# A decoder layer with 32 experts: the order of the last weight loads, and the final gate's product in split float32r terms

## The chip, the cores and the metric

The kernel runs on one core of a Trainium2 chip. The metric is device time of one launch in microseconds (us): 1184.36 us for the kernel before, the median of 3 runs (1183.37 to 1185.8). A lower number is better.

## The reference, cut to what matters

One decoder layer over 256 tokens of width 1024, all in float32. The change touches the last expert's second product and the last line, the gated embedding.

```python
D_MODEL = 1024; SEQ = 256; N_EXPERTS = 32; TOP_K = 4
h = x + mixer(rms_norm(x)) @ w_out                 # attention and recurrence, not touched here
m = rms_norm(h, ffn_norm_g)
for e in range(N_EXPERTS):                         # mixture of experts, added to h
    gu = m @ w_gu[e] + b_gu[e]                     # 1024 x 2048 weights
    gate = jnp.minimum(gu[:, :D_EXPERT], 7.0)
    up = jnp.clip(gu[:, D_EXPERT:], -7.0, 7.0)
    y = ((up + 1.0) * gate * jax.nn.sigmoid(1.702 * gate)) @ w_down[e] + b_down[e]
    out = out + gates[:, e:e + 1] * y              # gates is zero but for a token's four experts
h = h + out
h = h + (p @ W_ple) * jax.nn.sigmoid(h @ W_ple_gate)   # 256 x 1024 by 1024 x 1024
```

## The kernel before, in words

**The stream.** All large weights come through one list, `seq`, in pieces of 1 MB. SyncE (SP) issues one DMA for each piece, strictly in the order of the list (`fill`, L172), as soon as a buffer of the pool "slots" is free. For expert e the list holds eight pieces of gate-and-up weights ("GU", 128 rows x 2048 columns) and four of down weights ("D", two blocks of 128 x 1024). D of expert e-1 stands behind GU of expert e. At the end of the list stand GU of expert 31, D of expert 30, the four pieces of the final gate ("pg", four blocks of 128 x 512, in the order `GATE = [(0, 0), (1, 0), (0, 1), (1, 1)]` of column half and row half), and last D of expert 31:

```python
    expert("D", E - 2)
    for n, hf in GATE:
        add(("pg", n), hf, p_gate, 512 * n)
    expert("D", E - 1)
```

A piece is taken out by `need` and its buffer given back by `used`. Pieces of the mixer's weights are split on arrival into a high and a low float32r part (`split`: a ScalarE copy that rounds, L193, and a subtraction on VectorE or GpSimd, L194), and their products are three float32r matmuls (L380 to L382: high x high, low x high, high x low). GU, D and pg are used as they are, in float32; the trace has two matmul records for each of those matmuls.

**The experts.** Every expert has room for 64 tokens. `gate_up` (L1016) multiplies each GU piece as it lands; `hidden` transposes the result; `down` (L1047) multiplies each D piece as it lands, four matmuls of 64 x 512 a piece, for both column halves side by side on the array; ScalarE copies the sum out (`y`, L1051); `scatter` (L1058) adds it to the 256 tokens' accumulators `acc`, four matmuls. For expert 31 there is a function of its own, `last_down` (L1118, L1122): column half by column half, and inside one half in an order that takes rows of the first and the third D piece in turn, then of the second and the fourth.

**The end.** `final` adds `acc` to `h` (VectorE, L1129), transposes `h` with 128 x 128 matmuls (L1134), and ScalarE copies them to `fT` (L1135). `gate` multiplies `fT` with the pg pieces, 32 float32 matmuls of 128 x 512 (L1152). For each of the four output blocks of 128 x 512 follow a sigmoid (ScalarE, L1157), a product with the projected embedding `pp` (VectorE, L1158), a sum with `h` (L1159) and the DMA to the output (L1160), each in two halves of 256 columns.

The program is ordered by a scheduler with a timeline model, so instructions of one engine can stand in another order than the source has them; each engine then runs its own queue strictly in that order.

Of the kernel before, what the change touches and what calls it, by code (L numbers as in the profile page):

```python
# [11 lines left out]
F32 = mybir.dt.float32  # L12
F32R = mybir.dt.float32r
# [3 lines left out]
AF = mybir.ActivationFunctionType  # L17
OP = mybir.AluOpType
X = mybir.AxisListType.X

D = 1024
T = 256
E = 32
# [7 lines left out]
GATE = [(0, 0), (1, 0), (0, 1), (1, 1)]  # L31
# [5 lines left out]
def constants():  # L37
    P = np.arange(128)
    ident = np.eye(128, dtype=np.float32)
    t = np.arange(256)  # L40
    dl = t[:, None] - t[None, :]
    c = ((dl >= 0) & (dl <= 128)).astype(np.float32)
    for dil in (4, 16):
        c += ((dl >= 0) & (dl % dil == 0)).astype(np.float32)
    logc = np.where(c > 0, np.log(np.maximum(c, 1.0)), NEG).astype(np.float32)
    am = np.concatenate([logc[:128, :128], logc[128:]], axis=1)
    hm = []
    for L in (64, 32, 16, 8, 4, 2, 1):
        s, q = P[:, None], P[None, :]
        hm.append((s // (2 * L) == q // (2 * L)) & (s % (2 * L) < L) & (q % (2 * L) >= L))  # L50
    hm.append(P[:, None] == P[None, :])
    hm = np.concatenate([m.astype(np.float32) for m in hm], axis=1)
    tri = (P[:, None] < P[None, :]).astype(np.float32)
    half = 8
    inv = (500000.0 ** (-np.arange(half, dtype=np.float32) / np.float32(half))).astype(np.float32)
    inv = np.broadcast_to(inv, (128, 8))
    slot = np.broadcast_to(np.tile(np.arange(1, 65, dtype=np.float32), 2), (128, 128))
    sel = np.zeros((128, 32, 2), np.float32)
    for k in range(128):
        sel[k, k % 32, (k // 32) % 2] = 1.0  # L60
    sel = sel.reshape(128, 64)
    scan = np.ones((128, 1024), np.float32)
    scan[:, ::64] = 0.0
    parts = dict(ident=ident, inv=inv, am=am, hm=hm, tri=tri, slot=slot, sel=sel, scan=scan)
    at, off = {}, 0
    for n, a in parts.items():
        at[n] = (off, a.shape[1])
        off += a.shape[1]
    return at, np.ascontiguousarray(np.concatenate([np.asarray(a, np.float32) for a in parts.values()], axis=1))
# [41 lines left out]
def layer(ctx, tc, A, at):  # L111
    nc = tc.nc
    pe, act, dve, pool, sp = nc.tensor, nc.scalar, nc.vector, nc.gpsimd, nc.sync

    pers = ctx.enter_context(tc.tile_pool(name="pers", bufs=1))
    S = Slots(ctx.enter_context(tc.tile_pool(name="slots", bufs=N_SLOTS)), N_SLOTS)
# [8 lines left out]
    def add(name, hf, w, c=0):  # L125
        seq.append((name, hf))
        src[name, hf] = w[:, 4 * hf:4 * hf + 4, c:c + 512]
# [11 lines left out]
    def expert(kind, e):  # L139
        w, n = (w_gu, 8) if kind == "GU" else (w_dn, 4)  # L140
        for j in range(n):
            seq.append(((kind, e), j))
            src[(kind, e), j] = w[e, j]

    for e in range(E):
# [3 lines left out]
        if e == E_PLE:  # L149
            seq.append(("pj", 0))  # L150
            src["pj", 0] = A["ple_proj"][0].rearrange("(j p) n -> p j n", p=128)
    expert("D", E - 2)
    for n, hf in GATE:
        add(("pg", n), hf, p_gate, 512 * n)
    expert("D", E - 1)
    place = {k: i for i, k in enumerate(seq)}
    st = {"next": 0, "raw": 0, "cap": 0, "split": 0, "keep": 0}
    raw, parts, owner = {}, {}, {}
# [20 lines left out]
    def native(k):  # L179
        return k[0] == "pj" or k[0][0] in ("GU", "D", "pg")  # L180
# [17 lines left out]
    def ahead(name, hf, n):  # L198
        i = place[name, hf]
        while st["split"] < min(i + 1 + n, len(seq)):  # L200
            split(seq[st["split"]])
            st["split"] += 1

    def need(name, hf):
        ahead(name, hf, 0)
        r = parts.pop((name, hf))
        if native((name, hf)):
            owner[name, hf] = r[1]
        return r

    def used(name, hf, n=1):
        if native((name, hf)):
            S.free(1, owner.pop((name, hf)))
        st["raw"] -= 1
        ahead(name, hf, n)
        fill()


    h = S.new([128, 2, D], F32, "h")
# [50 lines left out]
    def bank():  # L270
        return ps.tile([128, 512], F32, name="bk", bufs=4)

    mm = misc = bank

    def pz():
        return ps.tile([128, 1024], F32, name="pz", bufs=2)
# [44 lines left out]
    for j in range(0, 8, 2):  # L321
        b = bank()
# [4 lines left out]
        for jj in range(2):  # L327
            s = b[:, jj * 256:jj * 256 + 256]
# [448 lines left out]
    for k in range(4):  # L777
        for g in range(2):
            c = g * D + (k % 2) * 512
# [47 lines left out]
    wp = ctx.enter_context(tc.tile_pool(name="work", bufs=1))  # L827
    R = {e: {} for e in range(E)}
    bgu = wp.tile([128, D], F32R, name="bgu")
    halves = (slice(0, 64), slice(64, 128))  # L830
# [174 lines left out]
    def gate_up(e, between):  # L1005
        G, U = mm(), mm()
        x = R[e]["x"]
        for k, P in enumerate((G, U)):
            pe.matmul(P, R[e]["sel"], bgu[:, k * 512:k * 512 + 512], start=True, stop=False,  # L1009
                      skip_group_check=True)  # L1010
# [28 lines left out]
    def down(e):  # L1039
        P = mm()  # L1040
        t = R[e]["h"]
        for j in range(4):
            w, _ = need(("D", e), j)
            for k in range(2):
                f = 2 * j + k
                for n in range(2):
                    pe.matmul(P[halves[n], :], t[:, f % 4, f // 4, :], w[:, k, n * 512:n * 512 + 512], start=f == 0, stop=f == 7,  # L1047
                              skip_group_check=True)
            used(("D", e), j, 0)
        y = wp.tile([128, 512], F32, name="y", bufs=2)  # L1050
        act.activation(y, P, AF.Copy)  # L1051
        R[e]["y"] = y

    def scatter(e):
        t, y = R[e]["ST"], R[e]["y"]
        for tt in range(2):
            for n in range(2):
                pe.matmul(acc[tt][n], t[halves[n], tt * 128:tt * 128 + 128], y[halves[n], :], start=e == 0, stop=False, skip_group_check=True)  # L1058

    acc2 = [pz(), pz()]  # L1060
    acc = [[acc2[n][:, tt * 512:tt * 512 + 512] for n in range(2)] for tt in range(2)]
# [13 lines left out]
    for e in range(E):  # L1075
# [22 lines left out]
        if e == E_SPILL:  # L1098
            overflow()
            st["keep"] -= 3  # L1100
            fill()
    scatter(E - 2)


    fT = S.new([128, 8, T], F32, "fT")
    sgs = S.new([128, 4, 512], F32, "sgs")

    def last_down(n):

        P = mm()  # L1110
        t = R[E - 1]["h"]
        for c in range(4):
            for k in range(2):
                f = 4 * k + c
                if (f // 2) not in last:
                    last[f // 2], _ = need(("D", E - 1), f // 2)
                w = last[f // 2]
                pe.matmul(P[halves[k], :], t[:, c, k, :], w[:, f % 2, n * 512:n * 512 + 512], start=c == 0, stop=c == 3, skip_group_check=True)  # L1118
        y = wp.tile([128, 512], F32, name="y", bufs=2)
        act.activation(y, P, AF.Copy)  # L1120
        for tt in range(2):
            pe.matmul(acc[tt][n], R[E - 1]["ST"][:, tt * 128:tt * 128 + 128], y, start=False, stop=True, skip_group_check=True)  # L1122

    last = {}

    def final(n):
        c = slice(n * 512, n * 512 + 512)
        for tt in range(2):
            dve.tensor_tensor(h[:, tt, c], h[:, tt, c], acc[tt][n], OP.add)  # L1129
        for j in (4 * n, 4 * n + 2):  # L1130
            b = misc()
            for k in range(2):
                for tt in range(2):
                    pe.transpose(b[:, k * 256 + tt * 128:k * 256 + tt * 128 + 128], h[:, tt, (j + k) * 128:(j + k) * 128 + 128], ident)  # L1134
            act.activation(fT[:, j:j + 2, :].rearrange("p j t -> p (j t)"), b, AF.Copy)  # L1135

    zp = {}

    def gate(n, hf):
        if not hf:  # L1140
            if n:
                zp[n] = [mm(), mm()]
            else:
                t = pz()
                zp[n] = [t[:, 0:512], t[:, 512:1024]]
        p = zp[n]
        w, _ = need(("pg", n), hf)
        for tt in range(2):
            s = slice(tt * 128, tt * 128 + 128)
            for jj in range(4):  # L1150
                j = 4 * hf + jj
                pe.matmul(p[tt], fT[:, j, s], w[:, jj, :], start=j == 0, stop=j == 7)  # L1152
            if hf:
                for c0 in range(0, 512, 256):
                    c = slice(n * 512 + c0, n * 512 + c0 + 256)
                    sg = sgs[:, 2 * n + tt, c0:c0 + 256]
                    act.activation(sg, p[tt][:, c0:c0 + 256], AF.Sigmoid)  # L1157
                    dve.tensor_tensor(sg, sg, pp[:, tt, c], OP.mult)  # L1158
                    dve.tensor_tensor(sg, sg, h[:, tt, c], OP.add)  # L1159
                    sp.dma_start(A["out"][0, tt * 128:tt * 128 + 128, c], sg)  # L1160

    last_down(0)
    last_down(1)
    final(0)
    final(1)
    for n, hf in GATE:
        gate(n, hf)


_INS = ["x", "p", "positions", "mix_norm_g", "w_in", "q_norm_g", "k_norm_g", "hgrn_lb_logits", "hgrn_norm_g", "w_out",  # L1170
# [20 lines left out]
```

## Time and profile before

| | us |
|---|---|
| median of 3 runs | 1184.36 |
| the profiled execution, whole time | 1185.23 |
| its span, first to last instruction | 1183.4 |
| DMA, mean over the span | 365 GB/s |
| PE busy (matmuls) | 1094.4 (92%) |
| VectorE busy | 284.0 (24%) |
| ScalarE busy | 195.1 (16%) |
| granted TensorE clock, mean | 0.98 |

The kernel moves 432 MB and spends most of its span on that: in the slices of the page between 240 us and 1125 us most show 415 to 418 GB/s. The time outside those slices is the mixer at the start and the tail after the last weights, and the change is all in the tail. Times below are us from the start of the span. PE is TensorE's matmuls, PEld its weight loads, ACT ScalarE, DVE VectorE, SPq SyncE's queue of DMA issues; "1.00" and "0.50" in a clock column are the 2.4 and the 1.2 GHz level.

### The profile page before, as it was taken

How to read it: one execution, taken by the hardware profiler on the slowest of the kernel's cores; microseconds unless marked ns; L12 is line 12 of the kernel's file. 1: busy time of each engine (PE TensorE's matmuls, PEld its weight loads, DVE VectorE, ACT ScalarE, POOL GpSimd, SP SyncE). 2: the span in 40 equal slices, each digit the busy share in tenths (PEclk: the TensorE clock that was granted, in tenths of full speed). 3: DMA queues.
4: the chain of work that ended last, by engine and by line, in shares of the span. 5: the costliest groups of instructions: out<-in, count | busy, mean ns of one | idle time of the engine just before them, and what ended most of it. 6: DMA issues, size and time to landing. Idle time of an engine off the chain costs nothing. (4 is left out here: it accounts for less than half of the span.)

```text
span 1183.4 us, 12240 instructions
## 1 busy us (share of the span) xinstructions
PE 1094.4 (92%) x4969; PEld 448.5 (38%) x4969; DVE 284.0 (24%) x601; ACT 195.1 (16%) x359; POOL 73.8 (6%) x77
## 2 busy tenths in 40 slices
PE   5899989999999999999999999899999999998778
PEld 4778764333333333333333322233333332222223
DVE  4878652211121111111112111001111211110001
ACT  5656531001010000000001000010001100000001
POOL 4432230000000000000000000000000000000000
PEclk9989997999999999999999999999999999999979
DMA  9913668999999999999999999999989999999941
GB/s 308 344 48 107 229 251 321 389 416 415 418 417 416 417 418 416 417 416 417 418 417 417 416 417 418 408 417 417 416 330 419 417 416 418 416 416 418 407 179 35
DMA packets 87117, 432.41 MB, mean 365 GB/s; under 512 B 7736, under 2 KB 9184, under 8 KB 54288
## 3 DMA queue, kind: packets, MB, share of 16 engines
q1 hardware_dynamic: 86480, 430.35, 90.1%
q0 software_dynamic: 576, 1.23, 0.4%
q8 instruction: 40, 0.66, 0.2%
q14 instruction: 21, 0.17, 0.0%
HBM read 430.51 MB, written 1.05 MB: 365 GB/s over the span
## 5 line engine op out<-in xcount | busy, mean ns | idle before, releaser
L1016 PE MATMUL bk<-raw,x 128*64 128x512 f32 x2048 | 476.1, 599 | 12.5 <-DMA raw<-in_expert_w_gate_up 12.3
L1016 PEld LDWEIGHTS bk<-raw,x 128*64 128x64 f32 x2048 | 143.5, 137 | 313.1 <-issue 264.3
L1047 PE MATMUL bk<-raw,ht 128*64 128x512 f32 x992 | 239.7, 598 | 10.4 <-DMA raw<-in_expert_w_down 10.3
L1047 PEld LDWEIGHTS bk<-raw,ht 128*64 128x64 f32 x992 | 69.0, 137 | 143.8 <-issue 112.2
L1023 DVE TENSOR_SCALAR gm<-bk 128x512 f32<-128x512 f32 x32 | 22.1, 691 | 365.2 <-PE bk L1016 365.2
L1024 ACT ACTIVATE sgm<-gm 128x512 f32<-128x512 f32 x32 | 20.2, 630 | 423.0 <-DVE gm L1023 423.0
L846 PE MATMUL bk<-h,sx 128*64 128x512 f32 x256 | 66.3, 616 | 9.5 <-ACT st L1002 9.5
L997 DVE TENSOR_SCALAR sg<-c_slot,posx,gates 128x128 f32<-128x128 f32 x64 | 19.3, 343 | 213.4 <-PE bk L1000 213.4
L1058 PE MATMUL pz<-y,st 64*128 64x512 f32 x248 | 64.6, 632 | 3.3 <-PEq L947 1.9
L838 POOL CAST sb<-c_sel 128x128 fp32r<-128x128 f32 x32 | 9.3, 293 | 848.6 <-PE bk L1009 834.2
L194 POOL TENSOR_TENSOR lo<-raw,hi 128x1024 fp32r<-128x1024 f32 x20 | 49.1, 2472 | 85.7 <-ACT hi L193 85.7
L859 DVE TENSOR_TENSOR x<-bk,gcol 128x256 f32<-128x256 f32 x64 | 24.2, 419 | 109.3 <-PE bk L855 109.3
L193 ACT ACTIVATE hi<-raw 128x1024 fp32r<-128x1024 f32 x36 | 37.8, 1056 | 23.5 <-issue 9.8
L1051 ACT ACTIVATE y<-bk 128x512 f32<-128x512 f32 x31 | 18.5, 597 | 134.2 <-PE bk L1047 134.2
L380 PE MATMUL pz<-hi,ahi 128*128 128x512 f32 x80 | 33.9, 423 | 6.5 <-DVE N L608 6.2
L1058 PEld LDWEIGHTS pz<-y,st 64*128 64x128 f32 x248 | 22.4, 192 | 44.8 <-issue 41.6
L835 DVE TENSOR_SCALAR sx<-c_slot,posx,rstd 128x64 f32<-128x64 f32 x64 | 17.2, 312 | 80.1 <-PE bk L846 80.0
L848 ACT ACTIVATE xr<-bk 128x512 f32<-128x512 f32 x32 | 19.1, 597 | 94.8 <-PE bk L846 94.8
L382 PE MATMUL pz<-hi,alo 128*128 128x512 f32 x80 | 33.2, 416 | 0.0
L381 PE MATMUL pz<-lo,ahi 128*128 128x512 f32 x80 | 33.1, 414 | 0.0
L846 PEld LDWEIGHTS bk<-h,sx 128*64 128x64 f32 x256 | 17.4, 139 | 38.7 <-issue 24.4
L1002 ACT ACTIVATE st<-bk 128x256 f32<-128x256 f32 x32 | 12.3, 384 | 116.0 <-PE bk L1000 116.0
(260 smaller groups left out, 837.8 us busy)
## 6 DMA issues: line engine op xcount, KB each, us to landing
raw<-in_expert_w_gate_up SPq DMA_DIRECT2D x256, 1024.0 KB, 19.9
raw<-in_expert_w_down SPq DMA_DIRECT2D x128, 1024.0 KB, 20.0
raw<-in_w_in SPq DMA_DIRECT2D x14, 1024.0 KB, 13.8
raw<-in_w_out SPq DMA_DIRECT2D x4, 1024.0 KB, 5.2
raw<-in_ple_gate SPq DMA_DIRECT2D x4, 1024.0 KB, 16.3
h<-in_x SPq DMA_DIRECT2D x2, 512.0 KB, 4.2
ct<-in_consts SPq DMA_DIRECT2D x2, 512.0 KB
raw<-in_ple_proj SPq DMA_DIRECT2D x1, 1024.0 KB, 20.6
```

Of the source, the lines that this page charges most:

```text
L193: act.activation(hi, w[:, o:o + 2], AF.Copy)
L194: (pool if i in POOL_FIRST else dve).tensor_tensor(lo, w[:, o:o + 2], hi.bitcast(F32), OP.subtract)
L380: pe.matmul(o, ahi[:, j, s], hi[:, jj, :], start=j == 0, stop=False)
L381: pe.matmul(o, ahi[:, j, s], lo[:, jj, :], start=False, stop=False)
L382: pe.matmul(o, alo[:, j, s], hi[:, jj, :], start=False, stop=j == 7)
L846: pe.matmul(b[halves[n], :], s[:, tt, :], h[:, tt, n * 512:n * 512 + 512], start=tt == 0, stop=tt == 1, skip_group_check=True)
L859: dve.tensor_tensor(x[:, :, n, :], b.rearrange("p (c n s) -> p c n s", c=4, n=2)[:, :, n, :], g, OP.mult)
L1016: pe.matmul(P[halves[n], :], x[:, j % 4, j // 4, :], w[:, c:c + 512], start=False, stop=j == 7, skip_group_check=True)
L1023: dve.tensor_scalar(gm, G, 7.0, None, op0=OP.min)
L1024: act.activation(sg, gm, AF.Sigmoid, scale=1.702)
L1047: pe.matmul(P[halves[n], :], t[:, f % 4, f // 4, :], w[:, k, n * 512:n * 512 + 512], start=f == 0, stop=f == 7, skip_group_check=True)
L1058: pe.matmul(acc[tt][n], t[halves[n], tt * 128:tt * 128 + 128], y[halves[n], :], start=e == 0, stop=False, skip_group_check=True)
```

## The change

Two edits. The list of loads ends with D of expert 31 and then pg, where before pg stood ahead of D of expert 31; `last_down` is gone, and expert 31 goes through `down` and `scatter` like the others. And the gate's product is made as the mixer's products are: `final` stores the transposed `h` as a high part (ScalarE, L1121) and a low part (VectorE, L1122); the new `gate_split` does the same to each pg piece, in two halves (L1131, L1132); and `gate` issues three float32r matmuls (L1151 to L1153) where one float32 matmul stood.

```diff
     expert("D", E - 2)
+    expert("D", E - 1)
     for n, hf in GATE:
         add(("pg", n), hf, p_gate, 512 * n)
-    expert("D", E - 1)
...
     scatter(E - 2)
+    down(E - 1)
+    scatter(E - 1)
-    fT = S.new([128, 8, T], F32, "fT")
+    fhi = S.new([128, 8, T], F32R, "fhi")
+    flo = S.new([128, 8, T], F32R, "flo")
     sgs = S.new([128, 4, 512], F32, "sgs")
-    def last_down(n):
-        P = mm()
-        t = R[E - 1]["h"]
-        for c in range(4):
-            for k in range(2):
-                f = 4 * k + c
-                if (f // 2) not in last:
-                    last[f // 2], _ = need(("D", E - 1), f // 2)
-                w = last[f // 2]
-                pe.matmul(P[halves[k], :], t[:, c, k, :], w[:, f % 2, n * 512:n * 512 + 512], start=c == 0, stop=c == 3, skip_group_check=True)
-        y = wp.tile([128, 512], F32, name="y", bufs=2)
-        act.activation(y, P, AF.Copy)
-        for tt in range(2):
-            pe.matmul(acc[tt][n], R[E - 1]["ST"][:, tt * 128:tt * 128 + 128], y, start=False, stop=True, skip_group_check=True)
     def final(n):
...
-            act.activation(fT[:, j:j + 2, :].rearrange("p j t -> p (j t)"), b, AF.Copy)
+            o = fhi[:, j:j + 2, :].rearrange("p j t -> p (j t)")
+            act.activation(o, b, AF.Copy)
+            dve.tensor_tensor(flo[:, j:j + 2, :].rearrange("p j t -> p (j t)"), b, o.bitcast(F32), OP.subtract)
+    pg = {}
+    def gate_split(n, hf):
+        w, _ = need(("pg", n), hf)
+        hi = S.new([128, 4, 512], F32R, "ghi")
+        lo = S.new([128, 4, 512], F32R, "glo")
+        for o in (0, 2):
+            act.activation(hi[:, o:o + 2], w[:, o:o + 2], AF.Copy)
+            dve.tensor_tensor(lo[:, o:o + 2], w[:, o:o + 2], hi[:, o:o + 2].bitcast(F32), OP.subtract)
+        used(("pg", n), hf, 0)
+        pg[n, hf] = hi, lo
     def gate(n, hf):
...
-        w, _ = need(("pg", n), hf)
+        hi, lo = pg[n, hf]
         for tt in range(2):
             s = slice(tt * 128, tt * 128 + 128)
             for jj in range(4):
                 j = 4 * hf + jj
-                pe.matmul(p[tt], fT[:, j, s], w[:, jj, :], start=j == 0, stop=j == 7)
+                pe.matmul(p[tt], fhi[:, j, s], hi[:, jj, :], start=j == 0, stop=False)
+                pe.matmul(p[tt], fhi[:, j, s], lo[:, jj, :], start=False, stop=False)
+                pe.matmul(p[tt], flo[:, j, s], hi[:, jj, :], start=False, stop=j == 7)
...
-    last_down(0)
-    last_down(1)
     final(0)
+    gate_split(*GATE[0])
     final(1)
-    for n, hf in GATE:
-        gate(n, hf)
+    for k in GATE[1:]:
+        gate_split(*k)
+    for k in GATE:
+        gate(*k)
```

SP's queue at the end of the list, before (-) and now (+); `raw` is a weight buffer, `sgs` the output block:

```order
 L172 DMA raw<-in_expert_w_gate_up 128x2048 x8
-L172 DMA raw<-in_expert_w_down 128x2x1024 x4
+L172 DMA raw<-in_expert_w_down 128x2x1024 x8
 L172 DMA raw<-in_ple_gate 128x4x512 x4
-L172 DMA raw<-in_expert_w_down 128x2x1024 x4
-L1160 DMA out<-sgs 128x256 x8
```

The four D loads of expert 31 moved ahead of the four pg loads; nothing else in this queue changed place.

TensorE's queue from the down product of expert 30 to the gate's first matmuls, before; `ht` is an expert's hidden activations, `st` its scatter matrix, `pz` and `bk` are PSUM tiles:

```order
L1047 MATMUL bk<-raw,ht 64x512 x12
L1058 MATMUL pz<-y,st 128x512 x4
L1118 MATMUL bk<-raw,ht 64x512 x16
L1122 MATMUL pz<-y,st 128x512 x4
L1134 MATMUL bk<-c_ident,h 128x128 x10
L1152 MATMUL pz<-raw,fT 128x512 x2
L1152 MATMUL bk<-raw,fT 128x512 x2
L1134 MATMUL bk<-c_ident,h 128x128 x6
L1152 MATMUL pz<-raw,fT 128x512 x6
```

The same place now; the last three rows go on in this manner, 96 matmuls in all:

```order
L1047 MATMUL bk<-raw,ht 64x512 x12
L1058 MATMUL pz<-y,st 128x512 x4
L1047 MATMUL bk<-raw,ht 64x512 x16
L1058 MATMUL pz<-y,st 128x512 x4
L1119 MATMUL bk<-c_ident,h 128x128 x16
L1151 MATMUL pz<-ghi,fhi 128x512
L1152 MATMUL pz<-glo,fhi 128x512
L1153 MATMUL pz<-ghi,flo 128x512
```

Expert 31's product became an ordinary `down`, all sixteen transposes now stand ahead of the gate, and each gate matmul became three.

ScalarE's queue behind the last sigmoid of the experts, now (before, three copies of a `y` and four of `fT` stood there ahead of the sigmoids):

```order
L1051 ACTIVATE y<-bk 128x512 x2
L1121 ACTIVATE fhi<-bk 128x512 x2
L1131 ACTIVATE ghi<-raw 128x1024 x2
L1121 ACTIVATE fhi<-bk 128x512 x2
L1131 ACTIVATE ghi<-raw 128x1024 x6
L1158 ACTIVATE sgs<-pz 128x256 x2
L1158 ACTIVATE sgs<-bk 128x256 x2
L1158 ACTIVATE sgs<-pz 128x256 x2
L1158 ACTIVATE sgs<-bk 128x256 x2
```

The splits of the pg pieces stand behind the copy of the last expert's `y` and between the copies of the transposed `h`.

VectorE's queue from behind the four sums into `h` (L1114, four of 128 x 512, as before) to the end, now:

```order
L1122 TENSOR_TENSOR flo<-bk,fhi 128x512 x2
L1132 TENSOR_TENSOR glo<-raw,ghi 128x1024 x2
L1122 TENSOR_TENSOR flo<-bk,fhi 128x512 x2
L1132 TENSOR_TENSOR glo<-raw,ghi 128x1024 x6
L1159 TENSOR_TENSOR sgs<-sgs,pp 128x256 x2
L1160 TENSOR_TENSOR sgs<-sgs,h 128x256 x2
L1159 TENSOR_TENSOR sgs<-sgs,pp 128x256 x2
L1160 TENSOR_TENSOR sgs<-sgs,h 128x256 x2
L1159 TENSOR_TENSOR sgs<-sgs,pp 128x256 x2
L1160 TENSOR_TENSOR sgs<-sgs,h 128x256
L1159 TENSOR_TENSOR sgs<-sgs,pp 128x256 x2
L1160 TENSOR_TENSOR sgs<-sgs,h 128x256 x3
```

Twelve subtractions came in between the sums and the output blocks; at the end the last two output blocks are handled together, where before each block's four instructions stood by themselves.

## Rows read from the trace of the kernel before

**Rows 1.** The chain in order of time, its last 100 us: start, us, what.

```profile
1120.92 15.34 DMA raw<-in_expert_w_down
...
1136.30 8.79 PE bk L1118 x28
1145.09 3.63 PE pz L1122 x8
...
1150.00 1.98 PE pz L1152 x4
...
1174.96 3.45 PE pz L1152 x8
```

**Rows 2.** Stages: from:to, length, busy time by engine, clock, DMA share, GB/s.

```profile
1110.20:1119.80 9.60, 8.29 (x36) 2.44 (x36) 1.45 (x3) 0.60 (x1) 0.00 (x0) 1.00 1.03 399
...
1136.30:1139.70 3.40, 3.40 (x8) 1.01 (x10) 0.00 (x0) 0.00 (x0) 0.00 (x0) 0.50 0.32 128
```

**Rows 3.** Timeline of SP's queue: DMA issues at the end of the list.

```profile
1090.20 10.00 SPq L172 DMA_DIRECT2D raw<-in_expert_w_down  x4
1100.30 16.68 SPq L172 DMA_DIRECT2D raw<-in_ple_gate  x4
1117.07 6.79 SPq L172 DMA_DIRECT2D raw<-in_expert_w_down  x4
```

**Rows 4.** Stages while pg pieces move, and while expert 31's D moves.

```profile
1117.00:1126.00 9.00, 4.13 (x18) 1.17 (x16) 0.00 (x0) 0.60 (x1) 0.00 (x0) 1.00 1.05 387
1128.00:1136.00 8.00, 3.65 (x4) 0.74 (x4) 0.00 (x0) 0.00 (x0) 0.00 (x0) 0.50 1.03 409
```

**Rows 5.** Timeline of TensorE: expert 30's first and last D piece, scatter, expert 31.

```profile
1110.23 1.94 PE L1047 MATMUL bk<-raw,ht 128*64 128x512 f32 x8 [0.70 <-DMA raw<-in_expert_w_down]
...
1117.85 1.94 PE L1047 MATMUL bk<-raw,ht 128*64 128x512 f32 x8 [0.64 <-DMA raw<-in_expert_w_down]
...
1120.48 1.99 PE L1058 MATMUL pz<-y,st 64*128 64x512 f32 x8 [0.70 <-ACT y L1051]
...
1131.27 3.65 PE L1118 MATMUL bk<-raw,ht 128*64 128x512 f32 x4 [8.81 <-DMA raw<-in_expert_w_down]
```

**Rows 6.** Timeline: the first sums into h, the first copies of fT.

```profile
1147.04 1.29 DVE L1129 TENSOR_TENSOR h<-h,pz 128x512 f32<-128x512 f32 x2 [35.26 <-PE pz L1122]
...
1149.35 1.08 ACT L1135 ACTIVATE fT<-bk 128x512 f32<-128x512 f32 x2 [3.57 <-PE bk L1134]
```

**Rows 7.** Splits in the mixer: group or line, count, ns min/median/max or mean.

```profile
L193 ACT ACTIVATE hi<-raw 128x1024 fp32r<-128x1024 f32 x36 | 37.8, 1056 | 23.5 <-issue 9.8 <-PE pz L381 8.8 <-DMA raw<-in_w_in 4.1
L194 DVE TENSOR_TENSOR lo<-raw,hi x16: 1206/1218/2922, 13.9 to 119.2; 128x1024 fp32r<-128x1024 f32 x16
L592 DVE TENSOR_TENSOR clo<-bk,chi 128x512 fp32r<-128x512 f32 x2 | 1.3, 686 | 0.5 <-ACT chi L591 0.5
L591 ACT ACTIVATE chi<-bk 128x512 fp32r<-128x512 f32 x2 | 1.1, 598 | 5.6 <-PE bk L584 5.6
```

**Rows 8.** Timeline of TensorE: float32r matmuls of the mixer, behind a pause.

```profile
72.40 0.76 PE L380 MATMUL pz<-hi,ahi 128*128 128x512 f32 x1 [2.90 <-DVE N L608]
72.96 0.63 PE L381 MATMUL pz<-lo,ahi 128*128 128x512 f32 x1
...
77.65 0.63 PE L380 MATMUL pz<-hi,ahi 128*128 128x512 f32 x1
...
78.39 0.40 PE L382 MATMUL pz<-hi,alo 128*128 128x512 f32 x1
...
79.79 0.40 PE L382 MATMUL pz<-hi,alo 128*128 128x512 f32 x1
```

**Rows 9.** Stage around that pause.

```profile
71.40:78.20 6.80, 5.80 (x14) 4.57 (x15) 6.73 (x17) 0.69 (x2) 0.00 (x0) 0.50 0.33 124
```

**Rows 10.** Timeline of the end: the last output block.

```profile
1178.85 0.76 DVE L1158 TENSOR_TENSOR sgs<-sgs,pp 128x256 f32<-128x256 f32 x2 [2.00 <-ACT sgs L1157]
1179.53 0.75 DVE L1159 TENSOR_TENSOR sgs<-sgs,h 128x256 f32<-128x256 f32 x2
```

More of the change, by code (lines that the diff above doesn't have):

```diff
@@ L1102, in layer @@
     scatter(E - 2)
-    fT = S.new([128, 8, T], F32, "fT")
+    down(E - 1)
+    scatter(E - 1)
+    fhi = S.new([128, 8, T], F32R, "fhi")
+    flo = S.new([128, 8, T], F32R, "flo")
     sgs = S.new([128, 4, 512], F32, "sgs")
-    def last_down(n):
-        P = mm()
-        t = R[E - 1]["h"]
-        for c in range(4):
-            for k in range(2):
-                f = 4 * k + c
-                if (f // 2) not in last:
-                    last[f // 2], _ = need(("D", E - 1), f // 2)
-                w = last[f // 2]
-                pe.matmul(P[halves[k], :], t[:, c, k, :], w[:, f % 2, n * 512:n * 512 + 512], start=c == 0, stop=c == 3, skip_group_check=True)
-        y = wp.tile([128, 512], F32, name="y", bufs=2)
-        act.activation(y, P, AF.Copy)
-        for tt in range(2):
-            pe.matmul(acc[tt][n], R[E - 1]["ST"][:, tt * 128:tt * 128 + 128], y, start=False, stop=True, skip_group_check=True)
-    last = {}
     def final(n):
```

## The prediction, made before the changed kernel ran

> **What bounds the kernel now.** I read the chain of waits first, from its end backwards, because only work on it moves the end. Its last large DMA link is the wait for the last expert's down weights, which ends at 1120.92 + 15.34 = 1136.26 [rows 1]. From there the chain is TensorE nearly all the way: 8.79 us of expert 31's down product, 3.63 of its scatter, then transposes and the gate, whose last eight records end at 1174.96 + 3.45 = 1178.41, and 5.0 us later the span is over at 1183.4. So the tail behind the last landing is 47.1 us. Next I read that tail by stages, for engines and clock [rows 2]. Up to 1119.8 TensorE follows the D pieces of expert 30 as they land, at the 2.4 GHz level (1.00). From the scatter's end at 1122.5 to 1131.27 it waits, 8.81 us at the last [rows 5], since the pg pieces that land then can't be used before h is finished. The stretch of half clock (0.50) that follows lasts until about 1139.7, over 3.4 us of gapless work from 1136.30 [rows 2]. And the order inside expert 31's product takes the first and the third piece in turn, so that only four records run before 1136.30 [rows 1, 5]. Meanwhile the DMA engines are full the whole time: 387 GB/s while pg moves, 409 while D moves [rows 4]. The stream can't be shortened by order, but what is left to do behind each landing can.
>
> **The change part by part.** All steps are made against the profiled execution, span 1183.4, whole time 1185.23, which is 0.87 above the median of the runs, 1184.36; I carry the difference over to that median.
>
> 1. *D ahead of pg.* Expert 30's last piece is multiplied from 1117.85, its first from 1110.23, so a piece comes every 2.54 us [rows 5]. A piece is 1.049 MB, at 409 GB/s 2.56 us [rows 4]. Four more end at 1117.85 + 4 x 2.56 = 1128.1, 8.2 earlier than 1136.3. The pg pieces follow at 387 GB/s, 2.71 us each, and land at 1130.8, 1133.5, 1136.2 and 1138.9. On SP's queue D 31 takes the places at which pg was issued, from 1100.30, and pg takes D's, from 1117.07 [rows 3]; no other DMA is moved past, and the outputs come far later.
>
> 2. *Expert 31 as an ordinary down.* Pieces 1 to 3 take 1.94 us each in a spacing of 2.56 and hide in the stream, as expert 30's did at full clock [rows 2, 5]. Behind the last piece the pattern of expert 30 holds: from its last piece to the scatter 1120.48 - 1117.85 = 2.63, the scatter 1.99 [rows 5]. 1128.1 + 2.63 + 1.99 = 1132.7. This 4.6 stands where 8.79 + 3.63 = 12.4 stood, a gain of 7.8.
>
> 3. *From the sums to the first float32r matmul.* The first sums into h start at once; from there to the first copy of the transposed h it was 1149.35 - 1147.04 = 2.31 [rows 6], so 1135.0 (TensorE was still busy with the scatter then, so this is rather long). Now the new waits. ScalarE's order is two copies, then the first half of the first pg piece: 2 x 0.60 + 1.06 = 2.26 [rows 7], 1137.3. VectorE then subtracts, 1.22 [rows 7], 1138.5; its two flo of 0.69 start behind the first copy and are over by 1137.0. The first matmul of the gate can go at 1137.3, the second, with glo, only at 1138.5, and the other 94 are queued behind it. Before, the gate began at 1150.0, 1.3 us behind the scatter [rows 1]; now it is 5.8: a loss of 4.5. The split has this price because all of it stands behind `y` in ScalarE's queue, though two pg pieces lie there earlier.
>
> 4. *The gate.* Before: 64 records at 3.45 / 8 = 0.431 [rows 1], 27.6 us. Now 96 float32r matmuls of the same shape as the mixer's, whose starts are (79.79 - 78.39) / 6 = 0.2333 apart at full clock [rows 8], each with a weight load of its own as there. From 1138.5: 94 x 0.2333 + 0.40 = 22.3, so 1160.8. The Trainium skill, page "FP8 and Floating Point Precision", section "TensorE Precision Notes", counts true FP32 as 4 passes through the array; with three one-pass terms the gate would by it be 27.6 x 3/4 = 20.7 and the whole 1.7 us earlier than by the rows. The row is a measured spacing of this very pattern, so the row is taken; the page does not name float32r.
>
> 5. *The other splits* cost nothing if they stay ahead of TensorE. VectorE goes on behind 1138.5: the first piece's second half 1139.7, two flo 1141.1, then six halves of 1.22 until 1148.4. TensorE needs the second half of piece 1 at 1138.5 + 6 x 0.2333 = 1139.9, piece 2 at 1144.1 (there by 1143.5 in full), piece 3 at 1149.7, piece 4 at 1155.3. ScalarE needs the last pg piece at about 1143.8, 4.9 us behind its landing. Without that cover, each half at the longest 2.92 that the mixer shows [rows 7], VectorE would end near 1162 and the end come some 4 us later.
>
> 6. *The clock.* From 1130 to 1138.5 TensorE has only a scatter, sixteen transposes and one matmul. Rows that show what follows such a stretch: behind 2.90 us of waiting the float32r matmuls of the mixer ran at (77.65 - 72.96) / 11 = 0.4264 apart [rows 8], clock 0.50 until 78.2 [rows 9], so for 5.8 us of gapless work; behind the pause of 8.81 us it was 3.4 us of gapless work [rows 2]. A us at half clock loses 1 - 0.2333 / 0.4264 = 0.45. That is 1.5 to 2.6 us; nothing, if the clock does not fall; I take the middle of the two rows, 2.1. TensorE ends at 1162.9.
>
> 7. *The end.* Before, 5.0 us from the last matmul to the span's end. Now the last two matmuls close one block only 0.47 us behind the other, so VectorE has eight instructions where it had four: four took 1180.28 - 1178.85 = 1.43 [rows 10], so +1.43, less the head start 0.47: +1.0. 1162.9 + 6.0 = 1168.9.
>
> Sum: -8.2 - 7.8 + 4.5 - 4.0 (the gate 24.4 with the clock's share, against 1150.0 to 1178.4) + 1.0 = -14.5. 1184.36 - 14.5 = 1169.9.
>
> **The rivals.**
>
> *The clock holds.* Steps 1 to 5 and 7 without 2.1: 1167.8. For it: at expert 30's pieces TensorE worked 8.29 of 9.60 us and kept 1.00 [rows 2]. Against it: from 1130 to 1138.5 it works less than half of the time.
>
> *D 31 lands late.* If its pieces came at the pace at which the four loads in their places were issued, 16.68 / 4 = 4.17 us [rows 3], the last would land at 1134.5, and everything behind it 6.4 later: 1176.3. Against it: the DMA share was 1.03 to 1.05 while those loads moved [rows 4], so bandwidth and not the issue was the limit, and the change leaves the buffers that these issues wait for the same.
>
> *Slower: the clock stays at 1.2 GHz to the end.* Three terms are more matmuls, and their gain rests on 2.4 GHz. At 0.4264 the gate takes 94 x 0.4264 + 0.6 = 40.7 instead of 24.4, 16.3 more: 1186.2; if the last piece and the scatter (1.94 + 1.99) also run at half, 1190.1. It decides from (14.5 + 2.1) / 0.193 = 86 of the 96 matmuls on. Against it: both half-clock stretches behind a pause ended within 5.8 us of gapless work, and the gate is gapless.
>
> *The change does not do what it says*: pg or the splits end up behind the gate's other work and the gain of step 2 alone is left. The queues as built speak against it: no wait ahead of the gate is for a later landing.
>
> **How the numbers follow.** The sum as worked out, 0.77; the clock holds, 0.12; D 31 late, 0.06; slower, 0.03; not what it says, 0.02. Likeliest: 1169.9. Low end: 1167.8 less 1.3 for step 3 being shorter and the spread of runs, 1166.5. High end: a clock stretch as long as the longer row and a little more, +1.5, and D 31 at pg's rate and splits up to 2 us late, 1173.5. Between them lie the first two cases, some 0.85. About 0.2%, 2.4 us, is what a measurement of this kernel can tell from no change: faster by more than that 0.95, within it 0.02, slower 0.03.
>
> **What would show it.** Right: expert 31's last D piece is multiplied near 1128, the last scatter ends near 1132.7, the first glo matmul starts near 1138.5 and waits for VectorE, the gate's matmuls are 0.233 apart with no waits inside but for a first stretch at 0.43, and the last ends near 1163. Wrong: a wait of the gate for VectorE or ScalarE behind its first six matmuls (step 5); D 31 landing behind 1130 (step 1); half clock past 1144 (step 6); a spacing above 0.24 at full clock (step 4); over 6.5 us behind the last matmul (step 7).

## The result, and the profile after

The changed kernel takes 1166.97 us, median of 6 runs (1165.67 to 1169.96); the kernel before, run beside it, 1185.08 us (1183.37 to 1188.54). The ratio is 0.985 with a 95% interval of 0.983 to 0.987, so 18 us less; forecast were 14.5 less, 1169.9, and a range of 1166.5 to 1173.5 (the forecast started from 1184.36). The profiled execution of the changed kernel has 1167.22 us, its span 1165.4.

Launches differ by some us in when the last weights come, before anything that the change touches runs. So the tail is measured below from one landmark, the start of expert 30's last down piece, to the span's end: 1183.4 - 1117.85 = 65.55 us before [rows 5], 1165.4 - 1117.22 = 48.2 us after. That is 17.4 of the 18 us; the landmark itself stands 0.6 us earlier.

The chain in order of time of the changed kernel, its last 70 us (start, us, what), answers to [rows 1]:

```profile
1097.05 20.13 DMA raw<-in_expert_w_down
1117.22 1.37 PE bk L1047 x5
1118.60 15.93 DMA raw<-in_ple_gate
1134.64 0.59 ACT fhi L1121
1135.24 0.95 ACT ghi L1131
1136.21 1.24 DVE glo L1132
1137.49 0.50 PE pz L1152
...
1158.66 0.24 PE pz L1153
...
```

The 8.79 and 3.63 us of expert 31's product and scatter are gone from it. In their place stand a copy of h, a copy of the gate's weights and a subtraction, then the gate without a gap. Read the third line with care: it puts ScalarE's wait ahead of the copies of the transposed h, until 1134.53, down to a pg piece. But the copy listed behind it, at 1134.64, is the second one; the first started at 1134.15. What held the copies is settled by e1_order below. The stages of the changed kernel, and then its timeline, tell more (columns as in [rows 2] and [rows 5]):

```profile
1121.80:1129.50 7.70, 7.28 (x34) 2.09 (x32) 0.00 (x0) 0.00 (x0) 0.00 (x0) 1.00 1.03 397
1129.50:1137.50 8.00, 4.90 (x26) 2.58 (x26) 5.06 (x8) 3.95 (x7) 0.00 (x0) 1.00 0.97 359
1137.50:1159.30 21.80, 21.80 (x95) 17.75 (x95) 11.95 (x17) 7.98 (x14) 0.00 (x0) 1.00 0.08 25
1159.30:1165.40 6.10, 0.04 (x1) 0.00 (x0) 2.77 (x8) 0.84 (x4) 0.00 (x0) 0.85 0.26 86
```

```profile
1117.22 1.94 PE L1047 MATMUL bk<-raw,ht 128*64 128x512 f32 x8 [0.63 <-DMA raw<-in_expert_w_down]
...
1121.78 5.37 PE L1047 MATMUL bk<-raw,ht 128*64 128x512 f32 x24
1127.46 1.94 PE L1047 MATMUL bk<-raw,ht 128*64 128x512 f32 x8 [0.31 <-DMA raw<-in_expert_w_down]
...
1130.15 1.99 PE L1058 MATMUL pz<-y,st 64*128 64x512 f32 x8 [0.76 <-ACT y L1051]
1132.17 2.48 DVE L1114 TENSOR_TENSOR h<-h,pz 128x512 f32<-128x512 f32 x4 [20.99 <-PE pz L1058]
1132.91 0.44 PE L1119 MATMUL bk<-c_ident,h 128*128 128x128 f32 x2 [0.77 <-DVE h L1114]
...
1134.15 1.09 ACT L1121 ACTIVATE fhi<-bk 128x512 fp32r<-128x512 f32 x2 [4.05 <-DMA raw<-in_ple_gate]
...
1135.12 2.01 ACT L1131 ACTIVATE ghi<-raw 128x1024 fp32r<-128x1024 f32 x2
1136.21 2.36 DVE L1132 TENSOR_TENSOR glo<-raw,ghi 128x1024 fp32r<-128x1024 f32 x2
1136.23 0.50 PE L1151 MATMUL pz<-ghi,fhi 128*128 128x512 f32 x1 [0.65 <-ACT ghi L1131]
...
1137.49 0.50 PE L1152 MATMUL pz<-glo,fhi 128*128 128x512 f32 x1 [0.76 <-DVE glo L1132]
...
1158.96 0.39 PE L1153 MATMUL bk<-ghi,flo 128*128 128x512 f32 x1
...
1159.35 0.76 DVE L1159 TENSOR_TENSOR sgs<-sgs,pp 128x256 f32<-128x256 f32 x2 [3.56 <-ACT sgs L1158]
...
1161.03 1.09 DVE L1160 TENSOR_TENSOR sgs<-sgs,h 128x256 f32<-128x256 f32 x3
```

Three things are to be seen. The wait of 8.81 us and the half clock that came with it [rows 2, 4, 5] are gone: every stage stands at 1.00 until the gate is over (the last one, 0.85, has next to no work for TensorE). TensorE's waits are down to 0.31, 0.76, 0.77, 0.65 and 0.76 us. And the price of the split is plain: the first gate matmul waits for the copy of the pg piece (ScalarE, L1131), the second for its subtraction (VectorE, L1132).

### The profile page after: what moved, and what is told of

Read it like the earlier page. It is cut to its first block, busy times and chain, and to the rows that moved or that the text cites. A ratio compares the mean times of both kernels' runs of the same rounds, so it can differ in the third digit from the quotient of the medians.

```text
span 1165.4 us, 12337 instructions
## 1 busy us (share of the span) xinstructions
PE 1080.2 (93%) x5001; PEld 451.9 (39%) x5001; DVE 294.1 (25%) x613; ACT 201.9 (17%) x366; POOL 74.8 (6%) x77
## 5 line engine op out<-in xcount | busy, mean ns | idle before, releaser
L1047 PE MATMUL bk<-raw,ht 128*64 128x512 f32 x1024 | 247.2, 598 | 12.5 <-DMA raw<-in_expert_w_down 12.5
L1047 PEld LDWEIGHTS bk<-raw,ht 128*64 128x64 f32 x1024 | 71.4, 136 | 150.9 <-issue 115.0
L1058 PEld LDWEIGHTS pz<-y,st 64*128 64x128 f32 x256 | 22.6, 188 | 45.7 <-issue 40.9
L835 DVE TENSOR_SCALAR sx<-c_slot,posx,rstd 128x64 f32<-128x64 f32 x64 | 17.2, 312 | 79.0 <-PE bk L846 78.9
L846 PEld LDWEIGHTS bk<-h,sx 128*64 128x64 f32 x256 | 17.4, 139 | 38.6 <-issue 24.4
```

The source lines that it names most:

```text
L846: pe.matmul(b[halves[n], :], s[:, tt, :], h[:, tt, n * 512:n * 512 + 512], start=tt == 0, stop=tt == 1, skip_group_check=True)
```

## The experiments

Line numbers in a row are those of the kernel that the row comes from. Diffs stand against the changed kernel where nothing else is said. "Tail" is the stretch from expert 30's last down piece to the end of the span.

**e1_order: the order alone.** The new list and the ordinary `down`, with the gate in float32 as before.

```diff
-            o = fhi[:, j:j + 2, :].rearrange("p j t -> p (j t)")
-            act.activation(o, b, AF.Copy)
-            dve.tensor_tensor(flo[:, j:j + 2, :].rearrange("p j t -> p (j t)"), b, o.bitcast(F32), OP.subtract)
+            act.activation(fT[:, j:j + 2, :].rearrange("p j t -> p (j t)"), b, AF.Copy)
...
-                pe.matmul(p[tt], fhi[:, j, s], hi[:, jj, :], start=j == 0, stop=False)
-                pe.matmul(p[tt], fhi[:, j, s], lo[:, jj, :], start=False, stop=False)
-                pe.matmul(p[tt], flo[:, j, s], hi[:, jj, :], start=False, stop=j == 7)
+                pe.matmul(p[tt], fT[:, j, s], w[:, jj, :], start=j == 0, stop=j == 7)
```

> The order of loads and the ordinary down alone; the gate stays float32, without a split. Theory (the gain is mostly the order): expert 31's last D piece is multiplied 10.2 us behind expert 30's last, as in the changed kernel; the first copy of the transposed h comes 7 us behind that; the gate then starts at once, some 2.7 us sooner than with the split, and takes 64 records at 0.431 = 27.6 us and the last transposes, against 22; 5.0 us to the end. That gives about 15 us less than the kernel before, ratio near 0.987, some 3 us above the changed kernel. Rival (the gain is mostly the cheaper product): 4 to 8 us less than before, ratio 0.993 to 0.997.

Measured: 1172.06 us, ratio 0.989 (0.986 to 0.992), tail 51.0, which is 14.6 less than before, as expected. Its timeline from the copies of h on:

```profile
1119.75 1.94 PE L1047 MATMUL bk<-raw,ht 128*64 128x512 f32 x8 [0.63 <-DMA raw<-in_expert_w_down]
...
1136.68 1.08 ACT L1119 ACTIVATE fT<-bk 128x512 f32<-128x512 f32 x2 [4.05 <-PE bk L1118]
1137.33 1.98 PE L1136 MATMUL pz<-raw,fT 128*128 128x512 f32 x4 [0.19 <-ACT fT L1119]
```

The order is most of the gain. It also settles the odd link of the chain above. Here the same copy stands at the same place, 1136.68 - 1119.75 = 16.93 us behind the landmark (changed kernel: 1134.15 - 1117.22 = 16.93), and ScalarE has read no pg piece, so the transposes release it. In the changed kernel the copy waits for nothing more; the pg piece that its row names isn't what held it. So the way from expert 31's last piece over its scatter, the sums and the transposes to that copy, 1134.15 - 1127.46 = 6.7 us, still sets the gate's start, though the chain leaves it out.

**e2_split: the split alone.** The old list and `last_down`, with the three-term gate.

```diff
     expert("D", E - 2)
-    expert("D", E - 1)
     for n, hf in GATE:
         add(("pg", n), hf, p_gate, 512 * n)
+    expert("D", E - 1)
...
+    last_down(0)
+    last_down(1)
     final(0)
```

> The split gate alone; the loads in the old order, with the old last product of expert 31. Theory: nothing changes until the sums into h; the copies and the first split hold the gate back as in the changed kernel, so it starts some 5.3 us behind the first sums where the float32 gate started 3.0 behind them; its 96 matmuls take 22 where 28.4 stood; the end is 1 us longer. About 3 us less than before, ratio near 0.9975. Rival (mostly the cheaper product): 8 us or more less, ratio 0.993 or below.

Measured: 1182.4 us, ratio 0.9975 (0.9961 to 0.9989), tail 63.3, which is 2.3 less than before. A stage and two rows of TensorE:

```profile
1126.00:1139.60 13.60, 8.02 (x16) 2.03 (x18) 0.00 (x0) 0.00 (x0) 0.00 (x0) 0.50 0.77 306
```

```profile
1150.83 0.49 PE L1167 MATMUL pz<-ghi,fhi 128*128 128x512 f32 x1 [0.46 <-ACT ghi L1147]
...
1152.09 0.50 PE L1168 MATMUL pz<-glo,fhi 128*128 128x512 f32 x1 [0.77 <-DVE glo L1148]
```

The half clock is where it was before, so the old order makes it. The gate is 6.6 us shorter (28.4 before, 21.8 here from 1152.09), but it starts 3.2 us later against the landmark (1152.09 - 1116.72 = 35.4, before 1150.00 - 1117.85 = 32.2) and the end is 1.1 longer: 2.3 are left. Order and split give 14.6 + 2.3 = 16.9 apart and 17.4 together, so they hardly touch each other.

**e3_early and e4_pause: the splits ahead of the sums.** If the first pg piece, which lies there since about 1130 (in e3_early its copy starts 13.0 us behind the landmark, released by the landing), were split before VectorE's sums into h, the price of step 3 should fall. e3_early moves the first piece's split, e4_pause those of all four. Here is e3_early; e4_pause puts the whole loop there.

```diff
-    final(0)
     gate_split(*GATE[0])
+    final(0)
     final(1)
```

> The changed kernel with the split of the first pg piece written ahead of the sums into h instead of behind the first copies. Theory (step 3: the gate's start waits for that split, so what moves it sooner moves the end): the split is over early, but its two subtractions now stand ahead of the sums on VectorE and hold them until about 1.4 us later; the first glo matmul comes about 1.2 us sooner, and the end with it, ratio to the changed kernel near 0.999. Rival (the start does not set the end, because later splits or landings hold the gate up): the end stays, and waits appear behind the first 24 matmuls.

> The changed kernel with all four splits written ahead of the sums into h, which lengthens TensorE's thin stretch ahead of the gate: the copies of the transposed h wait in ScalarE's queue for the landing and the split of the last pg piece. Theory for the clock (step 6 failed because the pause was too short in this case, not because the rule of the mixer's pause is wrong): the gate starts 3.5 to 6 us later than in the changed kernel and its first stretch runs at the 1.2 GHz level, matmuls 0.43 apart for 3 to 6 us, so 5 to 9 us slower than the changed kernel. Rival (the clock does not fall in this tail): only the 3.5 to 6 us of the later start, all matmuls 0.228 apart.

e3_early measured 1169.59 us, ratio 0.986 (0.983 to 0.989), tail 49.2: 1.0 us longer than the changed kernel's, where 1.2 less were expected. e4_pause: 1176.97 us, tail 56.0, 7.7 longer, as expected. The timeline and two stages of e3_early:

```profile
1135.96 0.44 PE L1119 MATMUL bk<-c_ident,h 128*128 128x128 f32 x2 [2.23 <-DVE h L1114]
...
1138.39 0.63 PE L1152 MATMUL pz<-glo,fhi 128*128 128x512 f32 x1
1138.82 1.48 PE L1119 MATMUL bk<-c_ident,h 128*128 128x128 f32 x6
...
1139.95 0.77 PE L1153 MATMUL pz<-ghi,flo 128*128 128x512 f32 x1
```

```profile
1129.40:1137.40 8.00, 4.85 (x26) 2.01 (x22) 4.45 (x6) 2.85 (x4) 0.00 (x0) 1.00 1.04 383
1137.40:1140.80 3.40, 3.38 (x13) 2.63 (x12) 3.18 (x5) 3.40 (x6) 0.00 (x0) 0.50 0.28 108
```

The glo matmul did come 0.7 us sooner against the landmark (1138.39 - 1118.82 = 19.57, changed kernel 20.27). But the sums now stand behind two subtractions on VectorE, so TensorE waits 2.23 us where it waited 0.77. The clock fell 1.4 us after the end of that wait, and six transposes came in between the second and the third gate matmul, which now starts 21.13 behind the landmark (changed kernel 1137.83 - 1117.22 = 20.61). That is 0.5 of the 1.0 us; the 0.85 us at half clock that are left behind 1139.95 make some 0.4 more, at the price that e8_busy gives below. The timeline and a stage of e4_pause:

```profile
1136.40 0.44 PE L1119 MATMUL bk<-c_ident,h 128*128 128x128 f32 x2 [2.23 <-DVE h L1114]
...
1142.75 0.77 PE L1151 MATMUL pz<-ghi,fhi 128*128 128x512 f32 x1 [3.68 <-ACT fhi L1121]
...
1145.60 0.80 PE L1153 MATMUL pz<-ghi,flo 128*128 128x512 f32 x1 [1.66 <-DVE flo L1122]
1146.19 0.63 PE L1151 MATMUL pz<-ghi,fhi 128*128 128x512 f32 x1
...
1149.18 0.61 PE L1153 MATMUL bk<-ghi,flo 128*128 128x512 f32 x1
```

```profile
1142.75:1149.60 6.85, 5.19 (x11) 3.65 (x12) 4.59 (x6) 1.41 (x3) 0.00 (x0) 0.50 0.00 0
```

With waits of 3.68 and 1.66 us the clock falls at the gate's first matmul and stays down for 6.85 us; the eight matmuls from 1146.19 to 1149.18 are 0.43 apart, those behind 1149.6 0.23. This is the stretch that step 6 had put into the changed kernel.

**e8_busy: the price of the clock by itself.** e4_pause with four float32 matmuls of 128x512 ahead of the gate's first, so that TensorE has work where it waited 3.68 us. They are extra work: the gate's first matmul overwrites what they write. The diff stands against e4_pause.

```diff
+        if (n, hf) == GATE[0]:
+            for _ in range(4):
+                pe.matmul(p[0], ident, h[:, 1, 512:1024], start=True, stop=True)
```

> e4_pause with four float32 matmuls of 128 x 512 added in the gate's pause, into the PSUM tile that the gate's first matmul then overwrites, from rows of h that are ready; they fill most of the 3.7 us in which TensorE waited for the first copy of the transposed h. Theory (the idle pause is what drops the clock): the gate stays at 2.4 GHz, matmuls 0.228 apart from the start, and from expert 30's last D piece to the end it takes 1.5 to 3 us less than e4_pause's 56.0. Rival (the clock falls for another reason, or the gain is lost to the added matmuls): half clock in the same place, 56 us or more.

Measured: 1173.94 us, tail 54.1, 1.9 less than e4_pause although it does more. The time is as expected, but not the way to it: the clock was to stay up, and it fell. Its timeline and the stage of half clock:

```profile
1135.22 0.44 PE L1119 MATMUL bk<-c_ident,h 128*128 128x128 f32 x2 [2.25 <-DVE h L1114]
...
1138.10 4.91 PE L1149 MATMUL pz<-h,c_ident 128*128 128x512 f32 x8
...
1144.43 0.50 PE L1156 MATMUL pz<-ghi,flo 128*128 128x512 f32 x1 [0.95 <-DVE flo L1122]
```

```profile
1137.30:1140.70 3.40, 3.40 (x10) 1.85 (x9) 3.40 (x4) 2.80 (x4) 0.00 (x0) 0.50 0.20 74
```

It fell sooner than in e4_pause, at 1137.3, behind the wait of 2.25 us ahead of the transposes, and the half-clock time was spent on the last transposes and the added matmuls. This run therefore doesn't show that the idle pause of 3.68 us drops the clock; it does show what a us at half clock costs the gate. The gate's third matmul, where its gapless part begins, starts at the same place in both: 1144.43 - 1118.07 = 26.36 here, 1145.60 - 1119.23 = 26.37 in e4_pause. So the 1.9 us lie all behind it, and are what 1149.6 - 1145.6 = 4.0 us at half clock cost the gate, 0.47 each. Step 6 had put 0.45 on such a us.

**e5_tail: the order of the output blocks.** Both row halves of one column half are finished before the other column half begins, so only one block is left at the end.

```diff
-GATE = [(0, 0), (1, 0), (0, 1), (1, 1)]
+GATE = [(0, 0), (0, 1), (1, 0), (1, 1)]
```

> The changed kernel with the pg pieces and the gate in the order of column halves, so that the gate's last matmuls close one output block alone. Theory (step 7: two blocks closing 0.5 us apart make the end 1 us longer than before): last matmul to the span's end 5.0 us instead of 6.05, all else as in the changed kernel; from expert 30's last D piece to the end 47.1 us instead of 48.2 where the clock holds. Rival (the end is set by the output DMAs alone, not by VectorE): still 6 us.

Measured: 1165.76 us, ratio 0.982 (0.980 to 0.984), tail 47.2, 1.0 less than the changed kernel's. Its timeline at the end:

```profile
1159.59 0.39 PE L1153 MATMUL bk<-ghi,flo 128*128 128x512 f32 x1
...
1160.43 0.76 DVE L1159 TENSOR_TENSOR sgs<-sgs,pp 128x256 f32<-128x256 f32 x2 [1.29 <-ACT sgs L1158]
1161.10 0.75 DVE L1160 TENSOR_TENSOR sgs<-sgs,h 128x256 f32<-128x256 f32 x2
```

VectorE has four instructions behind the last matmul again and not eight, and the span ends 5.05 us behind TensorE (6.1 in the changed kernel): the term of step 7, taken away.

**e7_both: the end's order, and the early split without its wait.** e5_tail, and the first piece split ahead of the sums as in e3_early, but with its second subtraction on GpSimd, so that VectorE reaches the sums sooner.

```diff
-    def gate_split(n, hf):
+    def gate_split(n, hf, low=None):
...
-            dve.tensor_tensor(lo[:, o:o + 2], w[:, o:o + 2], hi[:, o:o + 2].bitcast(F32), OP.subtract)
+            (low or (dve, dve))[o // 2].tensor_tensor(lo[:, o:o + 2], w[:, o:o + 2], hi[:, o:o + 2].bitcast(F32), OP.subtract)
...
+    gate_split(*GATE[0], low=(dve, pool))
     final(0)
-    gate_split(*GATE[0])
```

> The order of e5_tail and the split of the first pg piece ahead of the sums into h, its second subtraction on GpSimd, so that VectorE loses at most one subtraction ahead of the sums. Theory (steps 3 and 7): the gate's third matmul starts some 18 us behind expert 30's last D piece instead of 20.5, and the end is 5.0 us long: 45 us from that piece to the span's end where the clock holds, 3 us less than the changed kernel, near 1164 us. Rival (the gate is held by the next wait anyhow, the subtractions on VectorE): a gain of the end's 1 us alone, near 1166.

Measured: 1164.9 us, ratio 0.982 (0.980 to 0.985), tail 45.7 (45 expected), 2.5 less than the changed kernel's. Rows of GpSimd and TensorE:

```profile
1130.89 2.45 POOL L1132 TENSOR_TENSOR glo<-raw,ghi 128x1024 fp32r<-128x1024 f32 x1 [109.57 <-ACT ghi L1131]
1131.77 0.44 PE L1119 MATMUL bk<-c_ident,h 128*128 128x128 f32 x2 [1.09 <-DVE h L1114]
...
1134.75 0.48 PE L1153 MATMUL pz<-ghi,flo 128*128 128x512 f32 x1
```

The third gate matmul starts 1134.75 - 1115.75 = 19.0 us behind the landmark (changed kernel 20.61, about 18 expected). The wait ahead of the transposes was 1.1 us here, and the clock held until the gate was over.

**e9_again, e10_best to e13_after: is the shorter tail a shorter launch?** e9_again, e11_after and e13_after are the changed kernel unchanged, e10_best and e12_best are e7_both unchanged.

> The changed kernel once more, for its clock and for where expert 30's last D piece is multiplied. Theory: that piece comes anywhere between 1116.5 and 1120 us from run to run, as in the five profiles so far, and from it to the end the kernel takes 48.2 us if the clock holds and some 49.5 to 51 if it falls ahead of the gate. Rival: the clock of this tail always holds, 48.2 us again, and all spread of the runs comes from ahead of the tail.

> The kernel of e7_both once more, beside the changed kernel on the same chip. If its gain over the changed kernel is in the tail, the stretch from the start of expert 30's last down piece to the end of the span is again about 45.7 us here and 48.2 us in the changed kernel, and the medians differ by 2 to 3 us (ratio to the kernel before 0.982 against 0.985). If the difference seen so far was the spread of what lies ahead of the tail, the two medians are equal within 1 us.

> The changed kernel itself, timed beside the version with the earlier first piece and the shortened end: 48.2 us from expert 30's last down piece to the end, a ratio of about 0.985 to the kernel before, and 2 to 3 us above the other kernel of this pair; equal to it within 1 us if the end counts for nothing in the median.

> The kernel of e7_both a third time, in a pair with the changed kernel. Its stretch from expert 30's last down piece to the end of the span was 45.67 and 45.63 us in two looks against 48.22, 48.22 and 48.23. If the run's spread ahead of that stretch (up to 5 us between looks) is all that hid the gain in the last pair, the stretch is again about 45.7 us and, over all the runs so far and these, the mean is 1 to 3 us below the changed kernel's. If the shorter end is paid back ahead of it, the mean is the same and the last down piece of expert 30 starts later here than in the changed kernel by some 2.5 us on the mean of the looks.

> The changed kernel beside it: 48.2 us from expert 30's last down piece to the end, 1165.5 to 1170 us in single runs, its mean 1 to 3 us above the other kernel's, or equal to it if the shorter end is paid back ahead.

| kernel | label | median us (runs) | ratio to before (95%) | landmark | tail |
|---|---|---|---|---|---|
| changed | first runs | 1166.97 (6) | 0.985 (0.983 to 0.987) | 1117.2 | 48.2 |
| changed | e9_again | 1168.11 (1) | | 1118.1 | 48.2 |
| changed | e11_after | 1167.31 (5) | 0.985 (0.984 to 0.986) | 1119.2 | 48.2 |
| changed | e13_after | 1169.67 (6) | 0.987 (0.985 to 0.989) | 1119.9 | 48.2 |
| e7_both | e7_both | 1164.9 (4) | 0.982 (0.980 to 0.985) | 1115.8 | 45.7 |
| e7_both | e10_best | 1167.85 (5) | 0.985 (0.983 to 0.987) | 1121.0 | 45.6 |
| e7_both | e12_best | 1165.08 (5) | 0.984 (0.982 to 0.986) | 1115.7 | 45.7 |

The tails repeat to 0.1 us, and the landmark moves by over 5. In all seven traces the clock held until the gate was over, so of the two cases of e9_again the second is the one that was seen. In the pair e10_best and e11_after the landmark hid the whole gain, so the 2 to 3 us expected there were missed. Over all runs in the table the mean is 1165.8 us for e7_both (14 runs, standard deviation 2.0) and 1168.0 for the changed kernel (18 runs, 1.9): 2.3 us less, with a 95% interval of about 0.9 to 3.7 if the runs are taken as independent. That agrees with the 2.5 us of the tails, but it is uneven: in the two pairs the means differ by 0.3 us (e10_best and e11_after) and by 4.1 (e12_best and e13_after). Nothing shows that the shorter end is paid back ahead of it: e7_both's landmark is 1117.5 on the mean, the changed kernel's 1118.6, though three and four traces that differ by up to 5 us can't exclude it. So e7_both is probably 0.2% faster than the changed kernel, and the difference is about as large as a measurement can tell. Most of the landmark's spread is there by the end of the mixer. Here are the first stage and one of the mixer's last matmuls in two launches of this same kernel, e12_best and then e10_best:

```profile
0.00:126.00 126.00, 105.18 (x607) 88.25 (x608) 91.84 (x172) 74.49 (x121) 45.94 (x29) 1.00 0.54 190
127.33 0.39 PE L382 MATMUL pz<-hi,alo 128*128 128x512 f32 x1
```

```profile
0.00:126.00 126.00, 104.23 (x583) 88.34 (x584) 92.22 (x167) 71.57 (x112) 44.58 (x28) 0.95 0.54 190
131.89 0.39 PE L382 MATMUL pz<-hi,alo 128*128 128x512 f32 x1
```

Of the 5.3 us between their landmarks, 4.6 are there at this matmul. The granted clock up to 126 us is 1.00 in the one and 0.95 in the other, and the landmark follows the time at half clock in that stretch over all fourteen traces: 1115.7 with none, 1115.8 to 1117.9 with 6.8 us, 1117.8 to 1119.9 with 10.2 us, 1121.0 with 13.7 us. Why the clock differs there from launch to launch isn't shown.

## Why the prediction was right, step by step

The time was in the range, 2.9 us below the point and 0.5 above the low end. The range reached so far down because of the rival "the clock holds", which had a chance of 0.12; the likeliest case, with 0.77, isn't what happened. From the landmark to the end the forecast has 1168.9 - 1117.85 = 51.05 us, this rival 48.95, and 48.2 were measured. Against the landmark, forecast and measured:

| step | forecast | measured |
|---|---|---|
| 1: expert 31's last down piece | +10.25 | 1127.46: +10.24 |
| 2: end of the last scatter | +14.85 | 1132.14: +14.92 |
| 3: first copy of the transposed h | +17.2 | 1134.15: +16.93 |
| 3: first gate matmul | +19.4 | 1136.23: +19.0 |
| 3: first glo matmul | +20.65 | 1137.49: +20.27 |
| 4: spacing of the gate's matmuls | 0.2333 | (1158.96 - 1137.49) / 94 = 0.2284 |
| 6: what half clock costs | 2.1 | 0 |
| 7: behind the last matmul | 6.0 | 6.1 |

The span ended at 1165.4 where the sum had put 1168.9. Of these 3.5 us, 2.1 are step 6, 0.5 the spacing of step 4, 0.4 step 3, and 0.6 the landmark itself, which stood at 1117.22 instead of 1117.85; step 7 gives back 0.1.

Step 1 was right: D of expert 31 lands at the stream's pace, and the rival in which it lands late fell. Step 2 was right at its end. In its middle it was not: I had pieces 1 to 3 spaced by 2.56, but TensorE came to the first of them late, from expert 30's scatter, found the second and the third there when their turn came, and took all three in one run of 5.37 us. It was busy 7.28 of 7.70 us up to 1129.5.

Step 3 named both new waits, and both are in the trace, 0.65 and 0.76 us, with the releasers that it gave. It was 0.4 long: the first copy stood 0.2 earlier, as its bracket had said, and the two copies of h with the pg copy behind them took 2.04 us instead of 2.26. Each copy took about as long as forecast, but starts some 0.1 us before the one ahead of it is over (two copies of 0.60 are a row of 1.09). e3_early and e7_both show that its price can be cut, but only together with VectorE's queue.

Step 4 took the mixer's spacing, 2% too long. By the Trainium skill, page "FP8 and Floating Point Precision", section "TensorE Precision Notes", four passes for float32 against three terms gave an estimate of 20.7 us for the gate. Measured are 21.86 from its second matmul to its end, 22.3 forecast from the row. The truth lies between, nearer to the row.

Step 5 was right: behind 1137.83 no gate matmul waits for anything. Step 7 was right, and e5_tail took the term away.

**Step 6 failed**, as the sum's mis-sized term: the rival "the clock holds", at 1167.8, is what happened. The price of a us at half clock was right (e8_busy: 0.47, put at 0.45); that there would be any was wrong. I compared the stretch from 1130 to 1138.5 with two stretches that have waits of 2.90 and 8.81 us [rows 5, 8], because TensorE would work there for less than half of the time. Measured, it was busy for 4.90 of the 8.00 us from 1129.5 to 1137.5, and its longest single wait was 0.77 us. With waits of 2.2 us and more in the same place, e3_early, e4_pause and e8_busy do show the half clock. The share of work over such a stretch, by which I had chosen the rows, doesn't tell the cases apart: e3_early was busy for 4.85 of the 8.00 us ahead of its fall, and the mixer of the kernel before for 6.09 of the 8.00 us ahead of the stretch of [rows 9]:

```profile
63.40:71.40 8.00, 6.09 (x52) 5.89 (x50) 7.52 (x14) 4.30 (x5) 4.99 (x3) 1.00 0.11 27
```

By the longest single wait this tail is unlike both rows that I set beside it. That the wait is the cause was only argued; the last section has the place that speaks against so simple a rule.

## What to carry to other kernels

What this kernel paid for was the work that had to follow the last landing (e1_order: 14.6 of the 17.4 us). At the end of a stream of loads, let the piece with the longest chain behind it land earlier, and the one with the shortest chain last. Moving a step ahead on one engine can turn a short wait of TensorE into a longer one with half clock behind it, as in e3_early, so write down each single wait of TensorE in the new order before taking a gain for granted. And a gain of 2 us in a tail that repeats to 0.1 us can be invisible in medians, when the part of the launch ahead of it varies by 5.

## What was not expected of the hardware

What stood ahead of each fall of the granted clock in this tail, up to the end of the gate, can be listed. Behind waits of up to 0.78 us (changed kernel, e1_order, e5_tail) and of 1.1 us (e7_both) it stayed at the 2.4 GHz level. With each fall to 1.2 GHz went a wait of 2.23 us or more: 2.23 in e3_early and 2.25 in e8_busy, with the fall 1.4 and 2.1 us after its end; 3.68 in e4_pause, with the fall at its end; 8.81 before and 8.86 in e2_split, with the fall inside it, at 1126. The reverse doesn't hold in these rows: e4_pause also has a wait of 2.23 us ahead of its transposes, and they ran at 1.00 for the 2.7 us that they took. What tells the two cases apart stays open.

Three float32r terms on parts that were split on the spot took 21.86 us where float32 took 28.4 (27.6 by its records alone, as six transposes stand between them), and of the splits (12 copies on ScalarE, 12 subtractions on VectorE) all but the first were hidden. The price was 2.7 us at the gate's start (20.27 against 1137.33 - 1119.75 = 17.58 in e1_order) and 1.1 at the end, the gain 28.4 - 21.86 = 6.5. So the split gained 51.0 - 48.2 = 2.8 us net behind the new order, and 2.3 behind the old.
